# Banded self-attention in a decoder trunk: split-operand scores, values one projection tile later, wider bias and normalisation

## The chip, the cores and the metric

The kernel runs on one core of one Trainium2 chip. The metric is the device time of one execution in microseconds (us), lower is better. Engines are named as in the profile: PE is TensorE's matmul and PEld its weight load, DVE is VectorE, ACT is ScalarE, POOL is GpSimd, SP is SyncE, which here issues most of the transfers.

## The reference

A two-layer decoder trunk over 256 tokens of width 2048: a convolution and state-space layer, then a layer with banded self-attention; each is followed by cross-attention into 256 memory tokens and a gated MLP. The change lies in the banded self-attention of the second layer, 32 query heads of 64 channels over 4 key and value heads:

```python
def swa_sink_attention(h, w_qkv, b_qkv, sinks, rel_bias, w_out):
    z = h @ w_qkv + b_qkv
    q, k, v = jnp.split(z, [...], axis=-1)          # 32 query heads, 4 kv heads, 64 each
    ...
    kb, vb = with_prev(k), with_prev(v)             # block of 128 keys and the one before
    s = jnp.einsum('bnqkgd,bnskd->bnkgqs', q, kb) * (HEAD_DIM ** -0.5)
    rel = qi + BLOCK - kj
    bias = rel_bias[t5_causal_bucket(rel)]          # per head, by distance
    valid = (rel >= 0) & (rel < WINDOW) & (blk * BLOCK + kj - BLOCK >= 0)
    s = jnp.where(valid, s + bias, NEG_INF)
    p = softmax(concat([s, sink]))[..., :-1]        # one learned sink per head
    o = jnp.einsum('bnkgqs,bnskd->bnqkgd', p, vb)
    return o.reshape(...) @ w_out
```

There are two blocks of 128 queries. The first sees 128 keys, the second 256, so a head has 384 score columns for each of the 128 query rows.

## The kernel before, in words

Activations stay on chip with channels on partitions and the 256 tokens along the free axis. Large products use split operands: a float32 value is rounded to a short format (F32R) as its high part, and the remainder, rounded too, is its low part. One matmul of F32R operands is one pass. `wload` (L78) fetches a weight tile of 128 output channels, casts its high part on ACT (L90) and subtracts the low part on DVE (L91). `mm` (L112) runs 16 matmuls of 512 columns with the high weights against both parts of the activation (`mm_hi`, L105), and 16 of 256 columns with the low weights (`mm_lo`, L110). `gemm` (L119) does this per projection tile: load, `mm_hi`, an optional `half(n)`, `mm_lo`, then `evac(n)` and `after(n)`. With `pre` and `late` it starts some tiles with all but the last `late` contraction slices and finishes them afterwards.

`odd_mixer` interleaves the attention with two such products. A projection tile n of `od_q` gives the queries of a pair of heads, n. In the order in which the work is written, tile n holds:

- `half(n)`: `transp(n-3)` transposes the normalised probabilities of pair n-3 on PE (L748), one bank per head, and copies each bank to SBUF on ACT (L751);
- `evac_q(n)`: adds the two halves of the projection (L160, L161), scales on POOL (L700) and adds the bias on ACT into the float32 query tile (L702);
- `scores(n-1)`: float32 matmuls of 64 rows, 256 columns for the second block (L716) and 128 for the first (L719), each of which is two instructions in the trace; then on DVE scale and bias (L721, L722), maxima (L725, L726), small operations with the sink (L728 to L730); on ACT the sink's exponential (L731) and four exponentials with their sums (L734); on DVE denominators (L735, L736) and four multiplications by them (L739);
- `values(n-3)`: float32 matmuls of the values with the transposed probabilities (L762), then a split on ACT and DVE (L74, L75) into an operand of the output projection.

The last pairs run beside the first tiles of the output projection `od_w_out`. Score, transpose and value banks all come from one PSUM pool:

```python
self.pm = pool("pm", 4, space=PSUM)
def bank(self):
    return self.pm.tile([P, 512], F32, name="m", tag="m")
```

A tile takes `bank()` twice in `transp`, twice in `scores` and once in `values`. `rel_bias_setup`, run before the first layer's cross-attention, writes a table of 384 biases per head to DRAM (`fd`), from which `scores` fetches 128 shifted rows per head (L711). A scheduler orders each engine's instructions from the order written and from what is ready by its own estimates; that order is fixed in the program.

Of the kernel before, what the change touches and what calls it, by code (L numbers as in the profile page):

```python
# [22 lines left out]
P = 128  # L23
# [13 lines left out]
class Trunk:  # L37
# [597 lines left out]
    def rel_bias_setup(self):  # L635

        nc, I = self.nc, self.I
        with self.tc.tile_pool(name="rb", bufs=1) as pool:
# [10 lines left out]
            self.fd = self.dp.tile([32, 384], F32, name="fd")  # L649
            nc.scalar.dma_start(self.fd, f)  # L650

    def odd_mixer(self, xs):
# [3 lines left out]
        with tc.tile_pool(name="att", bufs=2) as pool:  # L656
            kT = [pool.tile([P, T], F32, name=f"kT{j}", tag=f"kT{j}", bufs=1) for j in range(2)]
            vt = pool.tile([P, 2, T], F32, name="vt", tag="vt", bufs=1)

            def evac_k(n, ps):  # L660
                z = self.t1()
                self.add_halves(z, ps)
                nc.gpsimd.tensor_tensor(z, z, self.rbc, op=ALU.mult)
                nc.scalar.activation(kT[n], z, AF.Identity, bias=self.k_b[:, n:n + 1])
# [32 lines left out]
            def evac_q(n, ps):  # L697
# [3 lines left out]
                q = pool.tile([P, T], F32, name="q", tag="q", bufs=3)  # L701
                nc.scalar.activation(q.rearrange("p (b i) -> p b i", b=2)[:, :, ::-1], z.rearrange("p (b i) -> p b i", b=2), AF.Identity, bias=self.q_b[:, n:n + 1])  # L702
# [4 lines left out]
            def scores(j):  # L707
                q = qs.pop(j)
                k = kT[j // 8]
                bias = pool.tile([P, 2, T], F32, name="bias", tag="bias", bufs=3)  # L710
                nc.sync.dma_start(bias, AP(tensor=self.fd.tensor, offset=self.fd.offset + 2 * j * 384, ap=[[1, P], [384, 2], [1, T]]))  # L711
                s = pool.tile([P, 2, 384], F32, name="s", tag="s", bufs=3)
                ps = [self.bank() for _ in range(2)]
                for hd in range(2):
                    r = slice(64 * hd, 64 * hd + 64)
                    nc.tensor.matmul(ps[hd][:, 0:T], lhsT=q[r, P:], rhs=k[r, :], start=True, stop=True)  # L716
                for hd in range(2):
                    r = slice(64 * hd, 64 * hd + 64)
                    nc.tensor.matmul(ps[hd][:, T:T + P], lhsT=q[r, :P], rhs=k[r, :P], start=True, stop=True)  # L719
                for hd in range(2):  # L720
                    v.scalar_tensor_tensor(s[:, hd, :T], ps[hd][:, :T], 0.125, bias[:, hd, :], op0=ALU.mult, op1=ALU.add)  # L721
                    v.scalar_tensor_tensor(s[:, hd, T:], ps[hd][:, T:T + P], 0.125, bias[:, hd, P:], op0=ALU.mult, op1=ALU.add)  # L722
# [13 lines left out]
                v.reciprocal(de, de)  # L736
                for hd in range(2):
                    for blk, sl in ((0, slice(0, T)), (1, slice(T, 384))):
# [338 lines left out]
```

## Time and profile before

| | before |
|---|---|
| runs | 2848.18, 2846.25, 2845.36 us; median 2846.25 us |
| profiled execution, its own time | 2847.27 us |
| span of that profile | 2845.5 us |
| granted TensorE clock, mean | 0.994 of full |
| PE busy | 2805.7 us (99%) |
| banded attention with its q projection | about 1664 to 1793 us of the span |

The span is what the profile covers; the profiled execution's own time is 1.8 us longer. All starts in the profile are in us from the start of the span, and "line" is a line of the kernel. A row of the timeline gives start, length, engine, line, operation, tiles and count, and in brackets the idle time before it on its engine and what ended that. A row of grouped instructions ends with busy time and mean length in ns, then the idle time before. A row of waits gives total, count and longest.

### The profile page before, as it was taken

The page shows a single profiled execution, that of the slowest core. Times are in us where ns is not written, and L with a number is a line of the kernel's source. Part 1 is how long each engine was busy: PE and PEld are TensorE (multiplying, and loading weights), DVE is VectorE, ACT ScalarE, POOL GpSimd, SP SyncE. Part 2 cuts the span into 40 slices and gives each one's busy share as a digit, 9 for nine tenths or more (in the row PEclk, how much of TensorE's full clock was granted, in tenths as well). Part 3 has the DMA queues.
Part 4 walks back from the last instruction along what each step waited for, and adds up shares of the span by engine and source line. Part 5 has one row for each costly group of instructions (what it writes and reads, how often), then busy time and mean ns, then how long its engine had stood idle before and what let it go on. Part 6 is the DMA issues. An engine that isn't in the chain of part 4 may idle for free.

```text
span 2845.5 us, 43900 instructions
## 1 busy us (share of the span) xinstructions
PE 2805.7 (99%) x17155; PEld 2492.1 (88%) x17155; DVE 1952.9 (69%) x3171; ACT 1566.1 (55%) x2509; POOL 345.4 (12%) x382
## 2 busy tenths in 40 slices
PE   7999999999999999999999999999999999999998
PEld 6988989998998888888888888889888888888887
DVE  5878697866766666666666778776666666666666
ACT  5766766644654544545545566655555455454454
POOL 0000000001001311202102310000122012021121
PEclk8999999999999999999999999999999999999999
DMA  7555555555555545555455554455455454654544
GB/s 283 204 201 189 206 191 205 210 179 181 206 188 182 189 171 210 184 185 197 170 207 184 179 193 154 154 208 185 165 188 195 165 207 171 213 189 166 208 170 142
DMA packets 90081, 538.83 MB, mean 189 GB/s; under 512 B 10672, under 2 KB 17168, under 8 KB 38672
## 3 DMA queue, kind: packets, MB, share of 16 engines
q1 hardware_dynamic: 86080, 520.47, 52.1%
q10 hardware_dynamic: 3792, 15.55, 1.4%
q8 instruction: 134, 2.20, 0.3%
q14 instruction: 75, 0.61, 0.1%
HBM read 525.45 MB, written 10.53 MB: 188 GB/s over the span
## 4 chain that ended last, share of the span: by engine, by line
PE 93%; DVE 3%; DMA 2%; ACT 1%; issue 1%; SPq 0%; POOL 0%; DVEq 0%; ACTq 0%; POOLq 0%
PE ps L105 49%; PE ps L110 28%; PE ps L102 3%; PE ps L103 3%; PE ps L326 2%; PE ps L327 2%; PE ps L331 2%; DVE lo L91 1%; PE m L856 1%; DMA raw<-in_ev_u 1%; PE m L762 1%; ACT stmp L496 1%; ACT hi L90 0%; DMA s5p<-in_s5p 0%; PE m L748 0%
## 5 line engine op out<-in xcount | busy, mean ns | idle before, releaser
L91 DVE TENSOR_TENSOR lo<-raw,hi 128x1024 fp32r<-128x1024 f32 (+2 forms) x1033 | 1202.2, 1185 | 414.4 <-ACT hi L90 161.6
L105 PE MATMUL ps<-op,hi 128*128 128x512 f32 x6069 | 1466.6, 392 | 6.5 <-DVE rcol L212 5.4
L90 ACT CAST hi<-raw 128x1024 fp32r<-128x1024 f32 (+2 forms) x1033 | 1002.1, 983 | 825.1 <-PE ps L105 695.1
L105 PEld LDWEIGHTS ps<-op,hi 128*128 128x128 f32 x6069 | 1114.3, 189 | 225.5 <-ACT hi L90 5.6
L110 PEld LDWEIGHTS ps<-op,lo 128*128 128x128 f32 x6976 | 897.4, 191 | 37.8 <-DVE lo L91 6.1
L110 PE MATMUL ps<-op,lo 128*128 128x256 f32 x6976 | 918.2, 283 | 4.8 <-DVE lo L91 4.8
L102 PE MATMUL ps<-op,hi 128*128 128x256 f32 x907 | 223.2, 286 | 6.2 <-ACT hi L90 6.1
L172 POOL TENSOR_TENSOR acc<-acc,t 128x256 f32<-128x256 f32 x84 | 77.0, 917 | 1229.1 <-ACT t L174 1229.1
L103 PE MATMUL ps<-op,hi 128*128 128x256 f32 x907 | 221.5, 284 | 0.0
L102 PEld LDWEIGHTS ps<-op,hi 128*128 128x128 f32 x907 | 174.8, 193 | 9.4 <-ACT hi L90 7.8
L103 PEld LDWEIGHTS ps<-op,hi 128*128 128x128 f32 x907 | 174.9, 193 | 0.1
L160 ACT COPY t<-ps 128x256 f32<-128x256 f32 x232 | 85.9, 371 | 150.6 <-PE ps L110 149.7
L893 POOL TENSOR_TENSOR t<-t,rbc 128x256 f32<-128x256 f32 x88 | 68.8, 781 | 749.1 <-DVE t L161 721.2
L896 DVE SCALAR_TENSOR_TENSOR t<-t,ff_conv 128x255 f32<-128x255 f32 x88 | 43.0, 488 | 141.8 <-ACT t L895 141.8
L899 POOL TENSOR_TENSOR t<-t,rbc 128x256 f32<-128x256 f32 x88 | 109.2, 1241 | 216.4 <-ACT t L898 216.4
L496 ACT ACTIVATE stmp<-S,s_pw 128x256 f32<-128x256 f32 (+3 forms) x256 | 118.0, 525 | 27.7 <-DVE S L503 24.1
L68 DVE SCALAR_TENSOR_TENSOR op<-h,gains,op 128x256 fp32r<-128x256 f32 x96 | 67.8, 713 | 86.6 <-ACT op L67 86.4
L75 DVE TENSOR_TENSOR op<-t,op 128x256 fp32r<-128x256 f32 x104 | 43.9, 425 | 116.8 <-ACT op L74 116.7
L326 PE MATMUL ps<-hi,op 128*128 128x512 f32 x256 | 101.2, 395 | 2.2 <-ACT hi L90 2.1
L327 PE MATMUL ps<-hi,op 128*128 128x512 f32 x256 | 99.9, 390 | 0.0
L161 DVE TENSOR_TENSOR t<-ps,t 128x256 f32<-128x256 f32 x232 | 96.4, 416 | 0.0
L905 POOL TENSOR_TENSOR t<-t 128x256 f32<-128x256 f32 x88 | 67.0, 762 | 135.0 <-DVE t L161 134.7
(219 smaller groups left out, 1727.9 us busy)
## 6 DMA issues: line engine op xcount, KB each, us to landing
raw<-in_ff_gate SPq DMA_DIRECT2D x88, 1024.0 KB, 4.8
raw<-in_ff_up SPq DMA_DIRECT2D x88, 1024.0 KB, 4.8
raw<-in_ff_down SPq DMA_DIRECT2D x128, 704.0 KB, 4.0
raw<-in_xa_k SPq DMA_DIRECT2D x32, 1024.0 KB, 5.1
raw<-in_xa_v SPq DMA_DIRECT2D x32, 1024.0 KB, 4.9
raw<-in_xa_q SPq DMA_DIRECT2D x32, 1024.0 KB, 4.8
raw<-in_xa_o SPq DMA_DIRECT2D x32, 1024.0 KB, 4.8
raw<-in_ev_w_in SPq DMA_DIRECT2D x28, 1024.0 KB, 4.9
```

The costliest lines, as they stand in the source:

```text
L90: nc.scalar.copy(hi, s)
L91: nc.vector.tensor_tensor(lo, s, hi.bitcast(F32), op=ALU.subtract)
L102: nc.tensor.matmul(ps[:, :T], lhsT=hi, rhs=o[:, :T], start=k == 0, stop=False)
L103: nc.tensor.matmul(ps[:, :T], lhsT=hi, rhs=o[:, T:], start=False, stop=False)
L105: nc.tensor.matmul(ps, lhsT=hi, rhs=o, start=k == 0, stop=False)
L110: self.nc.tensor.matmul(ps[:, :T], lhsT=w[k][1], rhs=ops[k][:, :T], start=False, stop=k == K - 1)
L160: self.nc.scalar.copy(t, ps[:, T:])
L161: self.nc.vector.tensor_tensor(out, ps[:, :T], t, op=ALU.add)
L326: nc.tensor.matmul(ps[b], lhsT=o[:, b * P:(b + 1) * P], rhs=w[j][0], start=k == 0, stop=False)
L327: nc.tensor.matmul(ps[b], lhsT=o[:, T + b * P:T + (b + 1) * P], rhs=w[j][0], start=False, stop=False)
L496: nc.scalar.activation(tmp[:, x, :, p - p0, :], at(0, both, p), AF.Copy, scale=pw[:, x, k, 8 * b + p:8 * b + p + 1])
L899: nc.gpsimd.tensor_tensor(y, y, self.rbc, op=ALU.mult)
```

## The change

Queries and keys are stored as a high and a low part in F32R (the low part made on DVE), and each score block is three single-pass products instead of one float32 product: high with high, high with low, low with high. The bias table holds 768 numbers per head, laid out as the 384 score columns need them, so that bias and scale are one DVE operation per head. The reciprocals are laid out per head and column block, and one DVE multiplication normalises both heads. `values` follows one projection tile later (pair n-4 in tile n), the last pairs move in the output projection accordingly, and that projection holds back four slices instead of three.

```diff
@@ -646,22 +646,26 @@
             nc.tensor.matmul(ps[:32, :384], lhsT=rb, rhs=oh, start=True, stop=True)
             f = pool.tile([32, 384], F32, name="f")
             nc.vector.tensor_tensor(f, ps[:32, :384], mk, op=ALU.add)
-            self.fd = self.dp.tile([32, 384], F32, name="fd")
-            nc.scalar.dma_start(self.fd, f)
+
+            self.fd = self.dp.tile([32, 3, 256], F32, name="fd")
+            for c, off in enumerate((0, P, P)):
+                nc.scalar.dma_start(self.fd[:, c, :], f[:, off:off + 256])
 
     def odd_mixer(self, xs):
         nc, tc, I = self.nc, self.tc, self.I
         v = nc.vector
         o_ops = []
         with tc.tile_pool(name="att", bufs=2) as pool:
-            kT = [pool.tile([P, T], F32, name=f"kT{j}", tag=f"kT{j}", bufs=1) for j in range(2)]
+            kT = [pool.tile([P, 2, T], F32R, name=f"kT{j}", tag=f"kT{j}", bufs=1) for j in range(2)]
             vt = pool.tile([P, 2, T], F32, name="vt", tag="vt", bufs=1)
 
             def evac_k(n, ps):
                 z = self.t1()
                 self.add_halves(z, ps)
                 nc.gpsimd.tensor_tensor(z, z, self.rbc, op=ALU.mult)
-                nc.scalar.activation(kT[n], z, AF.Identity, bias=self.k_b[:, n:n + 1])
+                b = self.k_b[:, n:n + 1]
+                nc.scalar.activation(kT[n][:, 0, :], z, AF.Identity, bias=b)
+                v.scalar_tensor_tensor(kT[n][:, 1, :], z, b, kT[n][:, 0, :].bitcast(F32), op0=ALU.add, op1=ALU.subtract)
             kps = []
             w = []
             for n in range(2):
@@ -698,8 +702,12 @@
                 z = self.t1()
                 self.add_halves(z, ps)
                 nc.gpsimd.tensor_tensor(z, z, rbc, op=ALU.mult)
-                q = pool.tile([P, T], F32, name="q", tag="q", bufs=3)
-                nc.scalar.activation(q.rearrange("p (b i) -> p b i", b=2)[:, :, ::-1], z.rearrange("p (b i) -> p b i", b=2), AF.Identity, bias=self.q_b[:, n:n + 1])
+
+                q = pool.tile([P, 2, 2, P], F32R, name="q", tag="q", bufs=3)
+                b = self.q_b[:, n:n + 1]
+                z2 = z.rearrange("p (b i) -> p b i", b=2)[:, :, ::-1]
+                nc.scalar.activation(q[:, 0], z2, AF.Identity, bias=b)
+                v.scalar_tensor_tensor(q[:, 1], z2, b, q[:, 0].bitcast(F32), op0=ALU.add, op1=ALU.subtract)
                 qs[n] = q
 
             sm = {}
@@ -707,19 +715,17 @@
             def scores(j):
                 q = qs.pop(j)
                 k = kT[j // 8]
-                bias = pool.tile([P, 2, T], F32, name="bias", tag="bias", bufs=3)
-                nc.sync.dma_start(bias, AP(tensor=self.fd.tensor, offset=self.fd.offset + 2 * j * 384, ap=[[1, P], [384, 2], [1, T]]))
+                bias = pool.tile([P, 2, 384], F32, name="bias", tag="bias", bufs=3)
+                nc.sync.dma_start(bias.rearrange("p a (c i) -> p (a c) i", c=3), AP(tensor=self.fd.tensor, offset=self.fd.offset + 2 * j * 768, ap=[[1, P], [256, 6], [1, P]]))
                 s = pool.tile([P, 2, 384], F32, name="s", tag="s", bufs=3)
                 ps = [self.bank() for _ in range(2)]
+                for b, cols, n in ((1, slice(0, T), T), (0, slice(T, 384), P)):
+                    for x, y in ((0, 0), (0, 1), (1, 0)):
+                        for hd in range(2):
+                            r = slice(64 * hd, 64 * hd + 64)
+                            nc.tensor.matmul(ps[hd][:, cols], lhsT=q[r, x, b, :], rhs=k[r, y, :n], start=x == y, stop=x == 1)
                 for hd in range(2):
-                    r = slice(64 * hd, 64 * hd + 64)
-                    nc.tensor.matmul(ps[hd][:, 0:T], lhsT=q[r, P:], rhs=k[r, :], start=True, stop=True)
-                for hd in range(2):
-                    r = slice(64 * hd, 64 * hd + 64)
-                    nc.tensor.matmul(ps[hd][:, T:T + P], lhsT=q[r, :P], rhs=k[r, :P], start=True, stop=True)
-                for hd in range(2):
-                    v.scalar_tensor_tensor(s[:, hd, :T], ps[hd][:, :T], 0.125, bias[:, hd, :], op0=ALU.mult, op1=ALU.add)
-                    v.scalar_tensor_tensor(s[:, hd, T:], ps[hd][:, T:T + P], 0.125, bias[:, hd, P:], op0=ALU.mult, op1=ALU.add)
+                    v.scalar_tensor_tensor(s[:, hd, :], ps[hd][:, :384], 0.125, bias[:, hd, :], op0=ALU.mult, op1=ALU.add)
                 st = pool.tile([P, 5, 2, 2], F32, name="st", tag="st", bufs=3)
                 mx, nm, sums, es, de = (st[:, i] for i in range(5))
                 v.tensor_reduce(mx[:, 0, :], s[:, :, :T], axis=AX.X, op=ALU.max)
@@ -733,10 +739,12 @@
                     for blk, sl in ((0, slice(0, T)), (1, slice(T, 384))):
                         nc.scalar.activation(s[:, hd, sl], s[:, hd, sl], AF.Exp, bias=nm[:, blk, hd:hd + 1], accum_out=sums[:, blk, hd:hd + 1])
                 v.tensor_tensor(de, sums, es, op=ALU.add)
-                v.reciprocal(de, de)
-                for hd in range(2):
-                    for blk, sl in ((0, slice(0, T)), (1, slice(T, 384))):
-                        v.tensor_scalar(s[:, hd, sl], s[:, hd, sl], de[:, blk, hd:hd + 1], None, op0=ALU.mult)
+                rd = pool.tile([P, 2, 3], F32, name="rd", tag="rd", bufs=3)
+                v.reciprocal(rd[:, :, 2], de[:, 1, :])
+                v.reciprocal(rd[:, :, 0], de[:, 0, :])
+                v.tensor_copy(rd[:, :, 1], rd[:, :, 0])
+                s6 = s.rearrange("p a (c i) -> p (a c) i", c=3)
+                v.tensor_tensor(s6, s6, rd.rearrange("p a c -> p (a c)").unsqueeze(2).to_broadcast([P, 6, P]), op=ALU.mult)
                 sm[j] = s
 
             def transp(j):
@@ -765,18 +773,18 @@
             def after(n):
                 if n >= 1:
                     scores(n - 1)
-                if n >= 3:
-                    values(n - 3)
+                if n >= 4:
+                    values(n - 4)
 
             def half(n):
                 if n >= 3:
                     transp(n - 3)
             self.gemm(lambda n: I["od_q"][n], range(16), xs, KT, evac_q, half=half, after=after)
             evac, nxt = self.resid_evac(G_XA + 1)
-            halves = {0: lambda: (values(13), scores(15)), 1: lambda: values(14), 2: lambda: transp(15)}
+            halves = {0: lambda: (values(12), scores(15)), 1: lambda: values(13), 2: lambda: (values(14), transp(15))}
             ends = {0: lambda: transp(14), 1: lambda: None, 2: lambda: values(15)}
             transp(13)
-            self.gemm(lambda n: I["od_w_out"][n], range(16), _Lazy(o_ops), KT, evac, late=3, pre=3, half=lambda n: n in halves and halves[n](), end=lambda n: ends[n]())
+            self.gemm(lambda n: I["od_w_out"][n], range(16), _Lazy(o_ops), KT, evac, late=4, pre=3, half=lambda n: n in halves and halves[n](), end=lambda n: ends[n]())
         return nxt
 
 
```

## The prediction

> **What bounds the kernel now.** I read the page's busy shares and its chain of work first, then the sums by stretch for this stage, then the waits and the timeline of one steady projection tile.
>
> ```profile
> span 2845.5 us, 43900 instructions
> PE 2805.7 (99%) x17155; PEld 2492.1 (88%) x17155; DVE 1952.9 (69%) x3171; ACT 1566.1 (55%) x2509; POOL 345.4 (12%) x382
> ...
> PE 93%; DVE 3%; DMA 2%; ACT 1%; issue 1%; SPq 0%; POOL 0%; DVEq 0%; ACTq 0%; POOLq 0%
> ```
>
> PE carries the whole kernel, so an edit is worth what it takes from PE's own stream or from PE's waits. The stretches are cut where a projection tile's first matmul (L105) or its scores (L716) begin.
>
> ```profile
> 1663.70:1669.26 5.56, 5.56 (x34) 4.91 (x33) 3.14 (x5) 2.10 (x2) 0.00 (x0) 1.00 0.37 116
> 1748.57:1757.12 8.55, 8.55 (x59) 7.09 (x59) 6.83 (x20) 5.84 (x18) 0.74 (x1) 1.00 0.47 155
> ...
> PEld m L762 <- ACT pT L751: 4.7, 25, 0.3
> ```
>
> Columns: stretch, length, busy PE, PEld, DVE, ACT, POOL, clock, DMA. A bare projection tile takes 5.56 us, one with attention 8.55 us, at full clock. DVE is free for 8.55 - 6.83 = 1.72 us of it. The last row is this stage's one recurring PE wait: the value matmuls for the copy of the transposed probabilities on ACT. One steady tile shows where:
>
> ```profile
> 1745.91 0.82 PE L748 MATMUL m<-ident,s 128*128 128x128 f32 x6
> 1745.95 0.16 DVE L730 TENSOR_TENSOR st<-st,sinks 128x4 f32<-128x4 f32 x1
> 1746.16 1.05 ACT L90 CAST hi<-raw 128x1024 fp32r<-128x1024 f32 x1 [0.79 <-PE ps L105]
> 1746.48 2.16 PE L110 MATMUL ps<-op,lo 128*128 128x256 f32 x16
> 1747.12 0.20 ACT L731 ACTIVATE st<-st 128x4 f32<-128x4 f32 x1
> 1748.57 0.70 PE L716 MATMUL m<-kT,q 64*128 64x256 f32 x4
> 1748.98 0.82 ACT L751 COPY pT<-m 128x384 f32<-128x384 f32 x2
> 1749.48 0.19 PEld L762 LDWEIGHTS m<-pT,vt 128*64 128x64 f32 x2 [0.18 <-ACT pT L751]
> 1749.86 0.63 PEld L762 LDWEIGHTS m<-pT,vt 128*64 128x64 f32 x10 [0.18 <-ACT pT L751]
> 1750.66 3.97 PE L105 MATMUL ps<-op,hi 128*128 128x512 f32 x16
> ```
>
> The values begin at 1749.48, when the first of the two copies is out; they do two of twelve instructions, stand until the second copy ends (1748.98 + 0.82 = 1749.80), and go on at 1749.86. From first value to the next projection: 1750.66 - 1749.48 = 1.18 us. ACT comes to the copies late because L90 (from 1746.16) and the exponentials of the next pair (L731 onward) stand ahead of them.
>
> **The change part by part.** *Values one tile later.* What the values cost when their copies are long done is seen at the stage's end:
>
> ```profile
> 1805.20 0.88 PE L762 MATMUL m<-pT,vt 128*64 128x128 f32 x12
> 1806.00 0.38 PE L110 MATMUL ps<-op,lo 128*128 128x256 f32 x1
> ```
>
> That is 0.80 us, so the second wait costs 1.18 - 0.80 = 0.38 us. It falls in tiles 3 to 15: 13 x 0.38 = 4.9 us gained. The wait for the first copy does not go with it. Each tile takes five banks from the pool of four (two for transposes, two for scores, one for values), so the values' bank is the one into which this tile's first head was transposed, and it comes free with the same first copy. What is late next is therefore that copy, through the bank instead of through the data: the values still start no sooner than 1749.48 - 1748.57 = 0.91 us after the scores. Values of pair 12 move to the output projection, where they cost the same 0.80 us.
>
> *Scores in single passes.* Two tiles have scores with nothing waiting behind them; the S5 stage has a block of the new kind, six rounds of single-pass 256-column matmuls in separate row groups.
>
> ```profile
> 1674.92 0.70 PE L716 MATMUL m<-kT,q 64*128 64x256 f32 x4
> 1675.46 0.39 PE L719 MATMUL m<-kT,q 64*128 64x128 f32 x4
> 1675.77 0.30 PEld L105 LDWEIGHTS ps<-op,hi 128*128 128x128 f32 x2
> ...
> L110 PE MATMUL ps<-op,lo 128*128 128x256 f32 x6976 | 918.2, 283 | 4.8 <-DVE lo L91 4.8
> ...
> 210.54 0.98 PE L395 MATMUL m<-us,BT 32*128 32x256 f32 x24
> 211.45 0.50 PE L326 MATMUL ps<-hi,op 128*128 128x512 f32 x1
> ```
>
> Old scores: 1675.77 - 1674.92 = 0.85 us. New: also six rounds, two heads each in its own 64 rows, three of 256 and three of 128 columns. The S5 block takes 0.91 us with all six at 256; no row shows a split-operand matmul of 128 columns. In the tile above, sixteen 256-column matmuls of L110 span 2.16 us and one lasts 0.28, so they start (2.16 - 0.28)/15 = 0.125 us apart. If a 128-column round took half, the block is 0.91 - 3 x 0.063 = 0.72. If it took as long as the old two-pass rounds of L719 (1675.77 - 1675.46 = 0.31 for two, the change of mode included, so 0.155 at most), it is 0.91 + 3 x 0.03 = 1.00. The nearest row is L748, six 128-column matmuls with a weight load each in 1746.48 - 1745.91 = 0.57, 0.095 apiece; that gives 0.91 - 3 x 0.03 = 0.82, which I take, with 0.72 and 1.00 as ends. So 0.03 us per pair, and only where no values follow: tiles 1 to 3 and pair 15, 4 x 0.03 = 0.1 us. Behind the other twelve the 0.91 us of the bank hides it; above 0.91 the excess would count twelve times.
>
> Here a page speaks against the edit. The Trainium skill ("TensorE: Matmul & The Clock Gate", section "LDWEIGHTS (loading the stationary operand)") says a load's time follows its columns (P / 1.2 ns), not its rows. By it each 128-column round waits 107 ns for its weights instead of streaming for half a 256-column round. That estimate makes the block 0.86 us and the gain of 0.1 us about nothing; L748's 0.095 us agrees with it more than with the half.
>
> *DVE: the low parts, wider bias and normalisation.*
>
> ```profile
> L91 DVE TENSOR_TENSOR lo<-raw,hi 128x1024 fp32r<-128x1024 f32 x3 | 3.6, 1223 | 3.3 <-PE ps L110 3.3
> L739 DVE TENSOR_SCALAR s<-s,st 128x256 f32<-128x256 f32 x2 | 1.0, 496 | 0.0
> L721 DVE SCALAR_TENSOR_TENSOR s<-m,bias 128x256 f32<-128x256 f32 x2 | 0.8, 401 | 0.0
> ...
> L722 DVE SCALAR_TENSOR_TENSOR s<-m,bias 128x128 f32<-128x128 f32 x2 | 0.6, 276 | 0.0
> L739 DVE TENSOR_SCALAR s<-s,st 128x128 f32<-128x128 f32 x2 | 0.5, 274 | 0.0
> ...
> L736 DVE RECIPROCAL st<-st 128x4 f32<-128x4 f32 x1 | 0.2, 167 | 0.0
> ...
> L896 DVE SCALAR_TENSOR_TENSOR t<-t,ff_conv 128x255 f32<-128x255 f32 x88 | 43.0, 488 | 141.8 <-ACT t L895 141.8
> ```
>
> Bias: out 2 x (0.401 + 0.276) = 1.35; in two of 384 columns, 0.401 + (0.401 - 0.276) = 0.53 each, 1.05. Normalisation: out 2 x (0.496 + 0.274) = 1.54; in one of 768 columns, 0.92 at L91's 1.2 ns per column, 1.54 if the broadcast operand eats all of the saving; L91 is also a product of two full operands, so I take 0.92. A second reciprocal and a tiny copy add 2 x 0.17 = 0.34; the low part of q adds 0.49 (L896's kind). Net -0.30 - 0.62 + 0.34 + 0.49 = -0.1 us of DVE per tile, +0.5 at the upper end, inside the free 1.72 us: cost nothing, covered by PE. If DVE finished L730 later, the cover is ACT's L90: L730 ends at 1746.11 and L731 starts at 1747.12, so the chain may slip by 1.0 us before the copies move. The two extra instructions for k run once, beside 32 matmuls.
>
> *Transfers.* The table is written by three transfers on ACT's queue instead of one, and each bias is 384 KB in 512-byte pieces instead of 256 KB.
>
> ```profile
> raw<-in_od_q SPq DMA_DIRECT2D x16, 1024.0 KB, 4.8
> ...
> bias<-fd SPq DMA_DIRECT2D x16, 256.0 KB, 3.7
> ```
>
> A weight tile, larger and in 512-byte pieces too, lands in 4.8 us, so a bias lies between 3.7 and 4.8. It is issued as soon as one of three bias buffers is freed, pairs ahead of its use; a weight load that it holds up on SP's queue has room, since the cast L90 above waits for PE to free its buffer, not for the load. The table is written a whole layer before its use. Both edits are at nothing.
>
> *The start of the output projection.* Pair 13 is transposed at once there, its values split around one L105:
>
> ```profile
> 1793.58 1.31 DVE L739 TENSOR_SCALAR s<-s,st 128x256 f32<-128x256 f32 x4
> 1794.38 0.52 PE L748 MATMUL m<-ident,s 128*128 128x128 f32 x3
> ...
> 1797.25 0.43 PE L762 MATMUL m<-pT,vt 128*64 128x128 f32 x2
> 1797.61 0.50 PE L105 MATMUL ps<-op,hi 128*128 128x512 f32 x1
> ...
> 1798.84 0.70 PE L716 MATMUL m<-kT,q 64*128 64x256 f32 x4
> ```
>
> The values there take 1798.84 - 1797.25 = 1.59 us with one L105 in them (0.23 apart: 3.97 less 0.50, over 15), which is 0.56 more than 0.23 + 0.80; with pair 12, copied long before, in that place the 0.56 goes. Against it, the transposes can no longer start on head 0 at 1794.38 while head 1 is still being normalised (to 1793.58 + 1.31 = 1794.89, and 0.34 for the small operations now ahead): 0 to 0.8 us, taken at 0.3, since other L105 can stand in between. Holding four instead of three late slices moves matmuls, it adds none.
>
> **Sum.** 4.9 + 0.1 + 0.56 - 0.3 = 5.3 us, from a span of 2845.5 to 2840.2. The profiled execution took 2847.27 us in all, 1.0 above the median of the runs, 2846.25; off that median the forecast is 2841.0 us, 0.18% faster. A difference under about 0.2% (5.7 us) can't be told from none here, so the forecast lies just inside "same".
>
> **The rivals.**
> 1. *The copies come earlier.* If ACT does the copies ahead of the weight cast or the exponentials, the bank no longer binds and the values follow the scores at 0.82: 12 x 0.09 = 1.1 us more, and with no loss at pair 13 5.3 + 1.1 + 0.3 = 6.7: 2839.6 us. For it: L730 (1746.11) and L90's start (1746.16) are only 0.05 us apart, so a small shift can swap them. Against: a shorter tile brings L90 earlier, not later. Chance 0.25.
> 2. *Single passes are slow.* A block of 1.00 us passes the 0.91: 12 x 0.09 + 4 x 0.15 = 1.7, and the 0.1 is lost: 5.3 - 1.8 = 3.5, 2842.8 us. Chance 0.1.
> 3. *It doesn't do what it says.* If the values get the bank of the second head's transposes, they start with the second copy, at 1749.86, and the 4.9 is lost: 2845.9 us. Against: five of four in strict turn gives the first. Chance 0.12.
> 4. *Slower: DVE gets stuck on the low part of q.* It needs POOL's product and ACT's high part. Queued right behind L161 it stands until both are done:
>
> ```profile
> 1750.17 0.42 DVE L161 TENSOR_TENSOR t<-ps,t 128x256 f32<-128x256 f32 x1
> 1751.45 0.51 ACT L702 ACTIVATE q<-t,q_b 128x256 f32<-128x256 f32 x1 [0.31 <-POOL t L700]
> ```
>
> From 1750.59 to 1751.96, plus 0.49 of its own and 0.34 for the small ones: 2.2 us, and bias, maxima, L730, exponentials and copies queue behind it. 1.0 us of that is covered; with the normalisation saving nothing, 2.2 - 0.3 - 1.0 = 0.9 us falls on each of twelve tiles, 10.8 us against 5.3: 2851.8 us. It decides from L730 1.4 us later (1.0 covered, 5.3/12 gained). For it: the order on DVE is fixed. Against: DVE now mixes L721 and L739 of different pairs, so others can stand in that gap. Chance 0.08.
>
> **How the numbers follow.** The forecast has 0.45. Its own range is 3.6 to 6.2 us of gain (pair 13's 0 to 0.8, the block's ends, some waits not found), 2840.0 to 2842.7; about a third of it lies above 5.7. Faster by over 0.2%: rival 1 and that third, 0.42. Slower: rival 4, 0.08. Within 0.2%: the rest, 0.50. The range leaves out rival 4 and the far end of rival 1: 2837.5 to 2846.5.
>
> **What would show it.** The values' second wait gone and 12 instructions in 0.80 us; tiles of 8.17 us instead of 8.55; values still starting 0.91 us behind the scores, with the first copy as releaser (if 0.82, rival 1; if on the second copy, rival 3); a score block near 0.82 us; L730 within 1.0 us of its place. It is wrong if the tile stays at 8.55, if scores show over 1.0 us, or if DVE stands before the low part of q.

## The result, and the profile after

| | before | changed |
|---|---|---|
| runs, median | 2846.53 us (4 runs beside it) | 2863.87 us (2863.57 to 2864.27) |
| ratio | | 1.0061, 95% interval 1.0045 to 1.0077 |
| span of the profile | 2845.5 us | 2862.1 us |

The change made the kernel 17 us slower; 2841.0 us was forecast, within 2837.5 to 2846.5. Lines of the changed kernel are numbered anew: L704 POOL's product, L709 ACT's high part of q, L710 DVE's low part of q, L726 scores, L728 bias, L731 and L732 maxima, L734 to L736 small operations, L737 and L740 exponentials, L741 denominators, L743 to L745 reciprocals, L747 normalisation, L756 transposes, L759 copies of them, L770 values. L90, L91 (weight casts and subtractions), L105, L110, L160 and L161 are as before.

The page first: span, busy shares, and the shares of the chain of work.

```profile
span 2862.1 us, 43983 instructions
...
PE 2800.6 (98%) x17219; PEld 2489.8 (87%) x17219; DVE 1961.4 (69%) x3141; ACT 1563.3 (55%) x2509; POOL 349.8 (12%) x382
...
PE 87%; DVE 6%; ACT 3%; DMA 2%; issue 1%; POOL 0%; SPq 0%; DVEq 0%; ACTq 0%; POOLq 0%
```

PE has 5 us less to do than before (2805.7) while the span is 17 us longer: PE waits. The sums by stretch say where: from the first q tile to the last, then from there to the first undisturbed tile of the output projection; first the kernel before, then the changed one, with three steady tiles and twelve microseconds of the second stretch (columns as in the prediction).

```profile
1663.70:1784.81 121.11, 121.09 (x811) 101.26 (x809) 94.51 (x252) 80.99 (x212) 10.38 (x14) 1.00 0.46 159
1784.81:1816.99 32.18, 32.09 (x217) 26.34 (x217) 21.31 (x65) 18.72 (x50) 1.48 (x2) 1.00 0.28 99
```

```profile
1663.06:1793.97 130.91, 116.28 (x855) 99.32 (x853) 98.27 (x223) 77.61 (x210) 12.89 (x14) 1.00 0.47 158
1793.97:1833.45 39.48, 34.33 (x238) 28.27 (x237) 25.31 (x61) 20.41 (x55) 2.31 (x2) 0.91 0.24 90
...
1734.03:1762.75 28.72, 24.63 (x187) 20.93 (x187) 21.45 (x51) 16.85 (x49) 3.07 (x3) 1.00 0.46 152
...
1802.66:1815.04 12.38, 8.59 (x55) 6.33 (x55) 7.57 (x20) 6.32 (x18) 1.57 (x1) 0.72 0.36 142
```

The stage is 17.1 us longer, all of the loss: 9.8 in the q projection and 7.3 at the start of the output projection (one block of values, about 0.8 us, has moved from the first stretch into the second). The tiles now come in a cycle of three, about 9.5, 10.4 and 8.9 us long, in the mean 28.72/3 = 9.57 us instead of 8.55, with PE busy 8.21 of it. DVE is busy 7.15 us per tile, not much more than the 6.83 before, so its work alone does not fill the tile; its waits tell more. First PE and DVE in the changed kernel's stage, then DVE in the same stage before (total, times, longest):

```profile
PE m L770 <- ACT pT L759: 12.2, 12, 1.4
...
DVE st L741 <- ACT s L740: 21.2, 14, 3.4
DVE q L710 <- ACT q L709: 10.9, 14, 1.5
...
DVE lo L91 <- PE ps L110: 2.0, 3, 0.9
```

```profile
DVE lo L91 <- PE ps L110: 21.3, 14, 1.7
```

Before, DVE waited for PE: the buffers of the weights' low parts. Now it hardly does; it stands for ACT at two places in every steady tile, in all 21.2 us for the exponentials and 10.9 us for the high part of q. In the three steady tiles these are 4.3 and 2.2 us, which with the busy time of 21.45 make 27.95 of the 28.72 us. One lap of DVE and ACT (in the other two of the three, DVE stands 1.83 us for the exponentials and 0.53 or 0.54 for the high part):

```profile
1746.45 0.96 DVE L747 TENSOR_TENSOR s<-s,rd 128x768 f32<-128x768 f32 x1
1747.32 0.42 DVE L161 TENSOR_TENSOR t<-ps,t 128x256 f32<-128x256 f32 x1
1747.66 1.22 DVE L91 TENSOR_TENSOR lo<-raw,hi 128x1024 fp32r<-128x1024 f32 x1
1747.88 1.58 POOL L704 TENSOR_TENSOR t<-t,rbc 128x256 f32<-128x256 f32 x1 [8.75 <-DVE t L161]
...
1750.04 0.48 DVE L710 SCALAR_TENSOR_TENSOR q<-t,q_b,q 128x256 fp32r<-128x256 f32 x1 [1.17 <-ACT q L709]
...
1750.44 1.01 DVE L728 SCALAR_TENSOR_TENSOR s<-m,bias 128x384 f32<-128x384 f32 x2
...
1753.14 0.51 ACT L740 ACTIVATE s<-s,st 128x256 f32<-128x256 f32 x1 [1.93 <-DVE st L735]
1753.25 1.23 DVE L91 TENSOR_TENSOR lo<-raw,hi 128x1024 fp32r<-128x1024 f32 x1
...
1755.01 0.83 ACT L759 COPY pT<-m 128x384 f32<-128x384 f32 x2
1755.13 0.16 DVE L741 TENSOR_TENSOR st<-st 128x4 f32<-128x4 f32 x1 [0.66 <-ACT s L740]
...
1755.52 0.88 PE L770 MATMUL m<-pT,vt 128*64 128x128 f32 x12 [1.18 <-ACT pT L759]
...
1755.74 1.05 ACT L90 CAST hi<-raw 128x1024 fp32r<-128x1024 f32 x1
```

Read it as a ring. DVE normalises (L747), only then adds the halves of the next q (L161), does one subtraction (L91), stands until POOL and ACT have made the high part, makes the low part (L710), and only then comes to the biases of the pair before (L728), maxima and small operations. ACT starts the exponentials at 1753.14, having stood 1.93 us for them; DVE has one subtraction (L91) to do meanwhile and then stands; normalisation follows, and so on round. Behind the exponentials on ACT come the copies that PE's values wait for (1.18 us) and the second weight cast (L90, 1755.74). In the kernel before, both casts stood ahead of the exponentials (the prediction's timeline has the second L90 at 1746.16, L731 at 1747.12), and both subtractions ran while ACT made the exponentials and the copies, so that the denominators (L735) found the sums ready:

```profile
1744.32 1.05 ACT L90 CAST hi<-raw 128x1024 fp32r<-128x1024 f32 x1 [0.92 <-PE ps L105]
...
1747.77 2.36 DVE L91 TENSOR_TENSOR lo<-raw,hi 128x1024 fp32r<-128x1024 f32 x2 [1.66 <-PE ps L110]
...
1748.60 0.39 ACT L734 ACTIVATE s<-s,st 128x128 f32<-128x128 f32 x1
...
1750.05 0.16 DVE L735 TENSOR_TENSOR st<-st 128x4 f32<-128x4 f32 x1
```

### The profile page after: what moved, and what is told of

The parts are those of the page before. It is cut to its first block, busy times and chain, and to the rows that moved or that the text cites. A ratio compares the mean times of both kernels' runs of the same rounds, so it can differ in the third digit from the quotient of the medians.

```text
span 2862.1 us, 43983 instructions
## 1 busy us (share of the span) xinstructions
PE 2800.6 (98%) x17219; PEld 2489.8 (87%) x17219; DVE 1961.4 (69%) x3141; ACT 1563.3 (55%) x2509; POOL 349.8 (12%) x382
## 4 chain that ended last, share of the span: by engine, by line
PE 87%; DVE 6%; ACT 3%; DMA 2%; issue 1%; POOL 0%; SPq 0%; DVEq 0%; ACTq 0%; POOLq 0%
PE ps L105 46%; PE ps L110 27%; PE ps L102 2%; PE ps L103 2%; DVE lo L91 2%; PE ps L326 2%; PE ps L327 2%; PE ps L331 2%; ACT stmp L496 1%; ACT s L740 1%; PE m L864 1%; ACT hi L90 1%; DMA raw<-in_ev_u 1%; DVE stmp L500 1%; DMA kv<-kst 1%
## 5 line engine op out<-in xcount | busy, mean ns | idle before, releaser
L105 PE MATMUL ps<-op,hi 128*128 128x512 f32 x6069 | 1467.6, 392 | 7.4 <-DVE rcol L212 6.3
L91 DVE TENSOR_TENSOR lo<-raw,hi 128x1024 fp32r<-128x1024 f32 (+2 forms) x1033 | 1203.0, 1184 | 386.5 <-ACT hi L90 156.9
L90 ACT CAST hi<-raw 128x1024 fp32r<-128x1024 f32 (+2 forms) x1033 | 1002.2, 983 | 806.0 <-PE ps L105 675.8
L105 PEld LDWEIGHTS ps<-op,hi 128*128 128x128 f32 x6069 | 1115.3, 189 | 226.0 <-ACT hi L90 6.4
L110 PEld LDWEIGHTS ps<-op,lo 128*128 128x128 f32 x6976 | 896.9, 191 | 38.7 <-DVE lo L91 7.0
L110 PE MATMUL ps<-op,lo 128*128 128x256 f32 x6976 | 917.8, 283 | 5.6 <-DVE lo L91 5.6
L160 ACT COPY t<-ps 128x256 f32<-128x256 f32 x232 | 86.0, 371 | 149.1 <-PE ps L110 148.1
L161 DVE TENSOR_TENSOR t<-ps,t 128x256 f32<-128x256 f32 x232 | 96.3, 415 | 2.0 <-ACT t L160 2.0
```

The source lines that it names most:

```text
L90: nc.scalar.copy(hi, s)
L91: nc.vector.tensor_tensor(lo, s, hi.bitcast(F32), op=ALU.subtract)
L105: nc.tensor.matmul(ps, lhsT=hi, rhs=o, start=k == 0, stop=False)
L110: self.nc.tensor.matmul(ps[:, :T], lhsT=w[k][1], rhs=ops[k][:, :T], start=False, stop=k == K - 1)
L160: self.nc.scalar.copy(t, ps[:, T:])
L161: self.nc.vector.tensor_tensor(out, ps[:, :T], t, op=ALU.add)
```

## The experiments

Each is one kernel, against runs of the kernel before on the same chip (2846.2 to 2846.5 us median). "Tile" is the mean steady tile, from one projection's first matmul to the next.

| what | time, us | ratio, 95% interval | tile, us |
|---|---|---|---|
| values later, alone | 2841.80 | 0.9984 (0.9975 to 0.9994) | 8.18 |
| split scores, alone | 2864.53 | 1.0062 (1.0047 to 1.0077) | 9.77 |
| wide bias and normalisation, alone | 2843.34 | 0.9991 (0.9981 to 1.0000) | 8.31 |
| the change without split scores | 2839.68 | 0.9976 (0.9967 to 0.9986) | 8.12 |
| the change, low part of q made later | 2861.34 | 1.0054 (1.0039 to 1.0069) | 9.57 |
| before, plus an unused low part of q | 2846.57 | 1.0002 (0.9992 to 1.0011) | 8.54 |
| split scores without q's low part | 2842.00 | 0.9985 (0.9975 to 0.9994) | 8.17 |
| the change with five attention banks | 2878.34 | 1.0112 (1.0097 to 1.0127) | 9.58 |
| the change, DVE's order pinned | 2854.63 | 1.0029 (1.0018 to 1.0041) | 8.93 |
| before, unused low part put early | 2857.02 | 1.0037 (1.0023 to 1.0051) | 9.33 |
| before, a subtraction moved | 2848.74 | 1.0009 (0.9999 to 1.0018) | 8.55 |
| the change, ACT's casts first | 2843.80 | 0.9990 (0.9981 to 0.9999) | 8.16 |
| the same, pair 13 transposed later | 2844.73 | 0.9995 (0.9986 to 1.0003) | 8.16 |
| split scores alone, ACT's casts first | 2848.79 | 1.0008 (0.9999 to 1.0017) | 8.53 |
| before, second cast late | 2843.37 | 0.9988 (0.9978 to 0.9997) | 8.38 |

**Which part.** The three parts of the diff were put into the kernel before one at a time, and the split scores were taken out of the change.

> The kernel before with the values one projection tile later and nothing else (no split scores, no wide operations). Theory Q (the low part of q makes DVE stand, and the copies of the transposed probabilities come late): without a low part nothing stands; the second wait of the values goes, 13 x 0.38 us and 0.56 at the output projection, so about 5 us faster than before, values 0.91 us behind the first scores. Rival W (the one wide normalisation holds DVE and with it the projection's evacuation): the same, about 5 us faster, as nothing here is wide. Rival V (moving the values is itself harmful, since their bank is free only with this tile's first copy): 0 to 10 us slower, with waits of the values on that copy of 0.4 us or more per tile.

> The kernel before with the split operands for the scores and nothing else (values as before, four bias operations and four normalisations). Theory Q: DVE stands before the low part of q for 0.5 to 1.2 us per tile, the copies come later than before and the values wait longer than the 0.44 us per tile of before: 8 to 17 us slower. Rivals W and V: the low part lies in DVE's free 1.7 us, PE's score block is 0.83 instead of 0.85 us: within 1 us of before.

> The kernel before with the one-operation bias and normalisation (and their table and transfers) and nothing else. Theory Q: DVE has about 0.6 us less to do per tile, nothing stands, the values wait as before: within 1.5 us of before, a slower one only by the transposes of pair 13. Rival W: the addition of the halves stands behind the 0.96 us operation, the chain is late, 5 to 17 us slower. Rival V: within 1.5 us of before.

> The changed kernel without its split scores: float32 scores as before, with the values later and the wide operations. Theory Q: the loss goes; 3 to 6 us faster than before. Rival W: still 5 to 17 us slower than before. Rival V: still slower than before, by 5 us or more.

The split scores alone carry the whole loss. The other two parts gain, and together they make the fastest kernel of this study. The wide operations were expected to change nothing and came out 2.9 us faster, with an interval that ends at none; why was not tried.

**What of the split scores.** Four kernels: the low part of q moved out of `evac_q` to the head of `scores`; the kernel before with a low part that no matmul reads; two products instead of three, so that no low part of q is needed (this leaves out a third of the score matmuls too); five banks for the attention, one of them taken from the projections. The code shows the main lines of each.

```diff
 # the change, low part later: in scores(j) instead of evac_q(n)
+                v.scalar_tensor_tensor(q[:, 1], z2, qb, q[:, 0].bitcast(F32), op0=ALU.add, op1=ALU.subtract)
 # before, unused low part: in evac_q(n), into a tile of its own
+                v.scalar_tensor_tensor(ql, z, self.q_b[:, n:n + 1], q, op0=ALU.add, op1=ALU.subtract)
 # without q's low part
-                    for x, y in ((0, 0), (0, 1), (1, 0)):
+                    for x, y in ((0, 0), (0, 1)):
 # five banks (the first tiles take their fourth bank from the attention's pool)
-        self.pp = pool("pp", 4, space=PSUM)
-        self.pm = pool("pm", 4, space=PSUM)
+        self.pp = pool("pp", 3, space=PSUM)
+        self.pm = pool("pm", 5, space=PSUM)
```

> The changed kernel, with the low part of q written one projection tile later, at the head of scores() instead of in the projection's evacuation; the same operations. Theory loop (through DVE's order the low part ties the projection's evacuation to the softmax of the pair before it: exponentials, copies, weight cast, L160, L161, POOL, ACT, low part, bias, maxima, exponentials in one ring of 9 to 10 us per tile): the input is then long done, DVE doesn't stand, the ring is open, and the kernel gains what the other two parts gave, 5 to 8 us faster than before. Rival load (DVE simply has too much to do with the low part): still 10 us or more slower than before.

> The kernel before with a low part of q made on DVE in the projection's evacuation, which no matmul reads; scores in float32 as before. Theory loop: all of the loss is there although PE does what it did before: 14 to 20 us slower. Rival passes (the loss comes with the split matmuls, their weight loads and banks): within 2 us of before.

> The split scores alone on the kernel before, without the low part of q: two products, high q with high and low k. It leaves out the third product of the scores. Theory loop: no ring, PE's score block shorter by a third, but the values wait for the copies as before and eat it: 0 to 3 us faster than before. Rival passes: still 8 us or more slower.

> The changed kernel with five banks for the attention and three for the projections, so that the values' bank is not the one of this tile's transposes. Rival bank (PE loses the time because the values wait for a bank): the wait of the values on the copy goes, 10 us or more of the 17 come back. Theory loop: the ring runs over ACT, DVE and POOL without the bank, so PE waits for it elsewhere (transposes, the scores' banks), and under 4 us come back.

Without the low part of q the loss is gone. With a fifth bank the tile stays at 9.58 us: PE hardly waits at the values any more (0.8 us in all), but 12.8 us for the normalisation, ahead of the transposes. The total of 2878.34 us, 14 us more than the change, was expected by neither side and says little here, since this kernel reaches the first q tile 13.9 us later (at 1676.99 instead of 1663.06 us). The other two missed what theory loop expected, and are the useful ones. Each came out as its rival had it, but the unused low part speaks against load, and the two products against passes. The unused low part puts the same operation on DVE, 28.92 us of work in four tiles (7.23 each), and costs nothing. And moving the low part away from its wait changed next to nothing, as the sums by stretch and DVE's waits over three tiles of that kernel show:

```profile
1737.27:1765.99 28.72, 24.42 (x188) 20.95 (x186) 21.34 (x52) 16.86 (x49) 4.75 (x3) 1.00 0.46 152
```

```profile
DVE st L741 <- ACT s L740: 5.5, 3, 1.8
DVE op L75 <- ACT op L74: 1.5, 3, 0.5
```

Busy 21.34 and stands of 5.5 and 1.5 fill 28.34 of 28.72 us: the stand before the low part went, the one for the exponentials grew. So neither the operation nor its own wait is the loss. What set the kernels apart was the order of DVE's instructions: in the fast ones both subtractions (L91) stood between the small operations and the denominators, in every tile or, with the wide operations, without split scores and without q's low part, in every second; in the slow ones they never both stood there.

**The order, pinned.** These kernels change no operation. They add edges that only fix the order in which an engine issues: in the changed kernel, both subtractions for tile j+4 behind the small operations of pair j and ahead of its denominators; in the kernel before with the unused low part, the order of the slow kernel; and the kernel before alone, with one subtraction moved as there. In the code the names are written out and the loops over the pairs left out; `behind(a, b)` puts a behind b.

```diff
 # the change, DVE's order pinned
+                behind(subtract0[j + 4], small[j]); behind(denominators[j], subtract1[j + 4])
 # before, unused low part put early
+                behind(denominators[j], subtract0[j + 4]); behind(add_halves[j + 2], normalise[j])
+                behind(subtract1[j + 4], add_halves[j + 2]); behind(low[j + 2], subtract1[j + 4])
+                behind(bias[j + 1], low[j + 2])
 # before, a subtraction moved: the same without low, the biases behind subtract1
```

> The changed kernel with every operation kept, and DVE's order pinned: the two low parts of the next weights' halves (1.22 us each) stand together behind the small operations with the sink and ahead of the denominators, as in the kernel before. Theory order (the loss lies in the place of these two subtractions in DVE's stream, not in what the change added): DVE no longer stands for the exponentials, a steady tile takes 8.1 to 8.3 us instead of 9.57, and the time is that of the changed kernel without split scores (2839.7) or a little less, 2835 to 2842 us. Rival chain (the scores now need the low part of q, and that path through POOL, ACT and DVE is what PE waits for, wherever the subtractions stand): the low part now comes behind the normalisation, later than before, so PE waits before the scores and the time stays at 2855 us or more. Rival load (DVE has too much to do): busy time is unchanged, so the time stays at 2860 or more.

> The kernel before, with the low part of q made on DVE and read by no matmul (the kernel that ran at 2846.6 us), and with DVE's order pinned to that of the kernel with split scores alone: one weights' subtraction between the sum of the projection's halves and the low part of q, the low part ahead of the biases, the other subtraction alone ahead of the denominators. No operation is added or taken away. Theory order: tiles of 9.4 to 9.8 us, DVE standing 0.5 to 0.7 us for the exponentials and about 1.2 us for q's high part, 12 or 13 tiles by 0.9 to 1.2, so 2857 to 2864 us. Rival chain (PE's need of the low part makes the loss): scores are still made from the float32 query, so no loss, 2845 to 2849 us.

> The kernel before with nothing added, and one of the two weights' subtractions per tile pinned between the sum of the projection's halves and the biases of the pair before, the other alone ahead of the denominators. Theory order in its strong form (the place of the subtractions alone is enough): DVE stands about 0.7 us for the exponentials, and POOL's product takes 1.58 us instead of 0.74 beside the subtraction, but nothing on DVE waits for ACT's high part of q; per tile about 0.7 us more on the way round DVE and ACT, a tile of 8.5 to 9.3 us: 2846 to 2856 us. If it takes both, the subtractions' place and the low part's wait, the loss is under 0.2%: 2846 to 2851 us. Rival chain: 2845 to 2847 us.

Order alone makes a loss: 2857.0 us against 2846.6 for the same instructions in the other order. The edges fix DVE's order; the scheduler answered with another order on ACT too, with the copies ahead of the exponentials and one of the two casts ahead of q's high part. The sum by stretch and DVE's waits over three tiles of the low part put early:

```profile
1725.68:1753.66 27.98, 24.95 (x176) 21.36 (x174) 21.38 (x61) 16.94 (x48) 4.69 (x3) 1.00 0.41 143
```

```profile
DVE ql L707 <- ACT q L705: 3.5, 3, 1.2
DVE st L740 <- ACT s L739: 2.7, 3, 0.9
```

21.38 + 3.5 + 2.7 = 27.6 of 27.98 us: DVE sets the tile with its work and two stands on ACT, and PE is idle for 3.0. The subtraction moved without a low part behind it left the tile at 8.55, and its 2.5 us can't be told from none; my strong form, that the subtractions' place is enough, is not borne out. In that kernel ACT kept both casts ahead of the exponentials, so it differs from the one above in ACT's order as well as in the low part. Pinning DVE's order in the change gave back 9 us, not the 20 or more that the theory asked for. The reason is in its trace (lines are one higher: L91 cast, L92 subtraction):

```profile
DVE lo L92 <- ACT hi L91: 14.3, 9, 2.3
```

DVE's second subtraction waited for ACT's cast, up to 2.35 us, since in most tiles ACT still made that cast behind the exponentials and copies, and my edge held the denominators behind it.

**ACT's order.** So the casts were put first on ACT, in the whole change and in the split scores alone, with DVE left to the scheduler. The opposite was done to the kernel before. In a fourth kernel `transp(13)` moved into the output projection's first tile.

```diff
 # ACT's casts first
+                behind(cast1[j + 4], cast0[j + 4]); behind(exponentials[j], cast1[j + 4])
 # before, second cast late
+                behind(exponentials[j], cast0[j + 4]); behind(cast1[j + 4], exponentials[j])
 # pair 13 transposed later
-            halves = {0: lambda: (values(12), scores(15)), 1: lambda: values(13), 2: lambda: (values(14), transp(15))}
+            halves = {0: lambda: (values(12), transp(13), scores(15)), 1: lambda: values(13), 2: lambda: (values(14), transp(15))}
-            transp(13)
```

> The changed kernel with every operation kept and only ACT's order pinned: both casts of the next weights' high parts ahead of the pair's exponentials, as the kernel before has them; DVE's order is left to the scheduler, which then puts both subtractions behind the small operations by itself and the low part of q behind the normalisation. Theory cast (the second cast had fallen behind the exponentials and copies on ACT, so DVE had nothing to do during the exponentials and its subtraction came late; that one place makes the loss): tiles of 8.1 to 8.3 us, no stand of DVE before the low part, 2836 to 2842 us. Rival load and chain (too much DVE work, or a longer way to the scores): over 2850 us.

> As the kernel with ACT's order pinned, and the transposes of pair 13 moved from the head of the output projection into its first tile, behind that tile's twelve large matmuls (about 2.9 us later). Theory: PE waited 1.9 us for that pair's normalisation in the changed kernel, and the matmuls after it ran at a lower granted clock; if the wait is still there with the order pinned, 1.5 to 4 us less than the kernel with ACT's order pinned, 2833 to 2840 us; if the pinned order already removes the wait, the same within 1 us. Rival (the transposes, later, make the values of pair 13 late, which hold the first tiles of the output projection): 1 to 4 us more.

> The kernel before with the split scores alone (2864.5 us as the scheduler ordered it) and ACT's order pinned, both casts ahead of the exponentials. Theory cast: the loss of the split scores is all in that order, so 2843 to 2848 us, tiles of 8.5 to 8.6 us as before. Rival (split scores cost something of their own): 2852 us or more.

> The kernel before with no operation changed, and on ACT the second cast of the next weights' high part pinned behind the pair's exponentials instead of ahead of them. Theory cast: DVE's second subtraction now waits for a cast that comes after the exponentials and the copies, 1 to 2.3 us on DVE per tile, with the denominators behind it: tiles of 8.8 to 9.6 us, 2849 to 2860 us. Rival low part (without the low part of q in DVE's stream the place of the cast is harmless, PE's own work covers it): 2845 to 2848 us.

With that one rule for ACT's order the change goes from 2863.87 to 2843.80 us with every operation kept, and the split scores alone from 2864.53 to 2848.79. The tiles are as expected, the times 1.8 and 0.8 us above what was expected. Sums and timeline of the change with ACT's casts first (lines are a few higher: L92 cast, L93 subtraction, L163 sum of halves, L715 low part of q, L731 scores, L733 bias, L745 exponentials, L746 denominators, L752 normalisation, L764 copies, L775 values):

```profile
1730.12:1754.60 24.48, 24.43 (x188) 20.94 (x186) 21.15 (x52) 17.20 (x48) 2.21 (x3) 1.00 0.54 178
1662.29:1779.09 116.80, 115.68 (x855) 99.40 (x853) 97.71 (x225) 79.44 (x211) 10.38 (x14) 1.00 0.54 180
1779.09:1813.07 33.98, 32.12 (x238) 26.67 (x237) 23.77 (x59) 19.71 (x53) 1.48 (x2) 1.00 0.27 94
```

```profile
1725.98 1.05 ACT L92 CAST hi<-raw 128x1024 fp32r<-128x1024 f32 x1 [0.77 <-PE ps L107]
...
1727.04 0.49 ACT L745 ACTIVATE s<-s,st 128x256 f32<-128x256 f32 x1
...
1727.60 2.36 DVE L93 TENSOR_TENSOR lo<-raw,hi 128x1024 fp32r<-128x1024 f32 x2 [1.03 <-PE ps L112]
...
1728.39 0.91 PE L731 MATMUL m<-kT,q 64*128 64x256 f32 x12
...
1729.31 0.88 PE L775 MATMUL m<-pT,vt 128*64 128x128 f32 x12
...
1729.87 0.16 DVE L746 TENSOR_TENSOR st<-st 128x4 f32<-128x4 f32 x1
1729.94 0.42 DVE L163 TENSOR_TENSOR t<-ps,t 128x256 f32<-128x256 f32 x1
...
1730.51 0.74 POOL L709 TENSOR_TENSOR t<-t,rbc 128x256 f32<-128x256 f32 x1 [7.40 <-DVE rd L749]
...
1731.65 0.94 DVE L752 TENSOR_TENSOR s<-s,rd 128x768 f32<-128x768 f32 x1
...
1732.52 0.47 DVE L715 SCALAR_TENSOR_TENSOR q<-t,q_b,q 128x256 fp32r<-128x256 f32 x1
```

DVE is busy 21.15 us in three tiles, as in the slow kernel (21.45), and the tile is 8.16 instead of 9.57. Both subtractions cover the exponentials; the sum of the halves comes ahead of the normalisation instead of behind it, so POOL and ACT work on q while DVE normalises, and the low part finds its operands ready. DVE waits only for PE, 1.03 us, and PE is never idle: 24.43 of 24.48.

The late cast in the kernel before cost nothing, it even gained 3 us, which neither side expected. In its trace DVE does one subtraction among the small operations and one ahead of the denominators, and still waits for PE. The cast's place is thus enough to undo the loss but not to make it. That it needs the low part as well, which closes the ring from q back to the biases, fits all the runs; how much of it is the place on ACT and how much the place on DVE is not separated, since pinning one engine mostly made the scheduler reorder the other. The later transposes of pair 13 took away two waits of PE (0.98 and 0.86 us) and put one for the operands of the output projection (0.55) in their place, but PE's busy time from the last q tile to the first undisturbed tile rose from 32.12 to 33.58 us; the time didn't change measurably.

## Why the prediction was wrong

**The step that failed** is in the part on DVE: net -0.1 us of busy time per tile, "inside the free 1.72 us: cost nothing, covered by PE", and "the cover is ACT's L90". Its durations were near: L728 0.55 (forecast 0.53), L747 0.99 (0.92), L710 0.48 (0.49).

```profile
L728 DVE SCALAR_TENSOR_TENSOR s<-m,bias 128x384 f32<-128x384 f32 x32 | 16.4, 548 | 0.0
L747 DVE TENSOR_TENSOR s<-s,rd 128x768 f32<-128x768 f32 x16 | 15.9, 992 | 0.5
L710 DVE SCALAR_TENSOR_TENSOR q<-t,q_b,q 128x256 fp32r<-128x256 f32 x16 | 7.7, 484 | 10.9 <-ACT q L709 10.9
```

Busy time did not decide. Against the 8.16 us tile the free time is 8.16 - 7.15 = 1.0 us, and it is used up as soon as DVE stands longer than that for something other than PE. I counted the free time without asking what fills DVE while ACT makes the exponentials (both subtractions), and took for granted that the scheduler would leave them there, and the casts on ACT with them. It ordered both engines anew: the second L90 came behind the exponentials (1755.74 against 1753.14), and ACT stood 1.93 us for DVE, so nothing was covered there, and DVE stood 32.1 us in the stage for ACT. With the casts put back ahead of the exponentials and nothing else pinned, 20 us came back.

**Rival 4**, slower with a chance of 0.08, named the right instruction: DVE stuck on the low part, right behind the sum of the halves, with the biases queued behind it. That stand was there, 10.9 us in all, or 0.8 each of 14 times where it reckoned 1.37. Its price, 2851.8 us against the measured 2863.87, was wrong, since it let the subtractions go on covering the exponentials; the larger stand, 21.2 us, is not in it. And with the low part moved away from that place the tile stayed at 9.57.

**What was right, once the order is as before:** the steady tile, 8.17 forecast and 8.16 measured; values still 0.91 us behind the scores, measured 1729.31 - 1728.39 = 0.92; values without the second wait 0.80, measured 0.81 (1730.12 - 1729.31). Values later, alone, gained 4.4 us (2846.19 to 2841.80), where 4.9 + 0.56 was forecast for this part; the interval reaches from 1.7 to 7.1. The score block, from the changed kernel:

```profile
1674.28 0.91 PE L726 MATMUL m<-kT,q 64*128 64x256 f32 x12
1675.11 1.19 PE L105 MATMUL ps<-op,hi 128*128 128x512 f32 x4
```

1675.11 - 1674.28 = 0.83 us, forecast 0.82, so rival 2 is out. The estimate of 0.86 from the Trainium skill ("TensorE: Matmul & The Clock Gate", section "LDWEIGHTS (loading the stationary operand)") is 0.03 off, too little for this block to speak against it.

**Mis-sized besides:** the start of the output projection, forecast at -0.56 + 0.3. With ACT's casts first it takes 33.98 us against 32.18, 1.8 more. PE's busy time there is the same (32.12 and 32.09), with one more block of values in it; what came on top is PE's stands for the normalisations of pairs 13 and 14, 0.98 and 0.86 us. In the q projection PE stands 0.65 us for the first pair's normalisation and 0.30 before the first values, which the forecast doesn't have either. So the whole stage is 150.78 us against 153.29, 2.5 shorter and not 5.3, though the steady tile is as forecast. The change without split scores stays ahead (2839.68 against 2843.80 us, though the intervals of their ratios overlap): even in the good order no gain of the split scores shows.

In the chances, rival 1 and a third of the forecast's 0.45 make 0.40, not 0.42.

**Open:** why the scheduler chose another order for the split scores and not for the unused low part was not tried. Nor is the last 2.3 us of the split scores with ACT's casts first settled; its interval includes none.

## What to carry to other kernels

A covered operation is covered by instructions in a place, not by a share of busy time: for each engine that is nearly full, name what it does during each of its waits, and what happens if a scheduler moves that work. The sign to look for in the profile is an engine whose busy time and waits on a third engine add up to the tile while the bounding engine's own releases have vanished from its list of waits. If an edit adds a dependent operation to such an engine, fix the order of the work that fills its waits with it: here one rule of order on ACT was worth 20 us, more than any part of the diff gained.

## What the hardware showed that I had not expected

POOL's product of 128x256 takes 0.74 us beside a bias operation of DVE and 1.58 us when a weights' subtraction runs on DVE (rows at 1730.51 and 1747.88 above). The subtraction reads two operands in SBUF; the bias reads one of its two from PSUM. The Trainium skill ("GPSIMD Engine Reference", section "1. Specifications") says that POOL's SBUF interfaces contend with DVE instructions of two SBUF inputs; these rows agree. The 0.84 us lies on the ring, but only in one of the three tiles of the changed kernel's cycle; in the other two the product takes 0.74 and 0.75.

A wait of PE can cost twice. At the start of the output projection the changed kernel's PE stood 1.36, 1.88 and 1.92 us within 6 us:

```profile
1802.66 0.88 PE L770 MATMUL m<-pT,vt 128*64 128x128 f32 x12 [1.36 <-ACT pT L759]
1805.41 0.52 PE L756 MATMUL m<-ident,s 128*128 128x128 f32 x3 [1.88 <-DVE s L747]
...
1808.54 0.90 PE L756 MATMUL m<-ident,s 128*128 128x128 f32 x3 [1.92 <-ACT pT L759]
1809.10 4.19 PE L105 MATMUL ps<-op,hi 128*128 128x512 f32 x9
```

The granted clock over 1802.66 to 1815.04 was 0.72: 1.00 up to 1806.8 and 0.50 from there to 1813.6. Nine L105 took 4.19 us, 0.46 apart instead of 0.23; this is part of the 7.3 us lost there. With waits of 0.98 and 0.86 us at the same place (ACT's casts first) the clock stayed at 1.00. It need not be several waits: with DVE's order pinned in the change, PE stood once at this place, 1.93 us up to 1801.34, and the clock was 0.50 from 1802.7 to 1809.5. Nor is length alone enough: the split scores alone have a wait of 2.52 us, up to 1812.32, and the clock stayed at 1.00 around it. What decides between them was not tried.
